# Seven products of w_up: partial sums kept growing in one pair of PSUM banks

## The chip, the cores and the metric

The kernel runs on one core of a Trainium2 chip. The metric is the device time of one execution in microseconds, lower is better; three runs of the kernel before are given, and one profiled execution.

## The reference

One layer of a streaming encoder in float32, for 1024 positions after 16 meta tokens, width 1024. Attention, a convolution module and their merge come first (some 1050 us of the kernel, not touched by the change); then a gated MLP whose two branches run through a causal convolution of three taps:

```python
n2 = _rms(h, norm_ffn_w[l])
up = _causal_dwconv(n2 @ w_up[l], ffn_dw_w[l], ffn_dw_b[l])     # w_up: 1024 x 5632
gate, val = jnp.split(up, 2, axis=-1)
h = h + (jax.nn.silu(gate) * val) @ w_down[l]                   # w_down: 2816 x 1024
out = _rms(h, norm_final_w)
```

## The kernel before

Activations lie with features on the partitions. Each factor of a product is split into two float32r parts, high and low, and `mm3` (line 141) makes three matmuls of each product of parts (lines 143 to 145): high by high, low by high, high by low.

w_up has 44 column tiles of 128: 22 of the gate and 22 of the value. Tiles p and 22 + p are made as a pair. The first two pairs go by plain products; the other twenty (p = 2 to 21) by Winograd's form of Strassen's algorithm in `strassen` (line 920): w's two tiles are cut into four blocks by halves of the features (a11, a12, a21, a22), the activations into four by halves of the features and of the tokens (b11, b12, b21, b22), and seven products of blocks and of sums of blocks give four results: c11 and c12 (the gate, in the row tile u1), c21 and c22 (the value, u2). The sums s1 to s4 of w's blocks are made per pair by `seven` (line 894) on VectorE; t1 to t4 of the activations are made once.

`product` (line 839) makes one of the seven: 24 matmuls with 258 columns each, 12 into either of two PSUM banks. `banks` gives a pair of banks from a pool of four such pairs, so all eight banks are used in turn. In the program's names, `ps_u` is such a pair, and the second factor names the product: `b11h`/`b11l` for a11 b11, `t2h`/`t2l` for s2 t2, `b21` for a12 b21, `t3` for s3 t3, `b12` for a22 t4 (t4 lies where b12 was), `t1` for s1 t1, `b22` for s4 b22. `whi` and `wlo` are the two parts of w's blocks, made by a cast on ScalarE (line 688) and a subtraction on VectorE (line 689).

Each product has banks of its own. The first is copied to u1 on ScalarE (line 928), and VectorE adds the other six to rows of u1 and u2 in SBUF, in seven additions (line 926), since s1 t1 goes into two results. Then `act` (line 831) runs the convolution of three taps over u2 and u1 (`conv3`: one step on ScalarE, line 825, and two on VectorE, line 827, for each row), the SiLU on ScalarE (line 835), the product of gate and value on VectorE (line 836), and stores the result. Rows u1, u2 and the convolution's two rows come from one pool of four (`urow`), so the next pair's u1 and u2 take places that the pair before must have let go.

w_down follows, again in seven products by groups; its first blocks are loaded into places that w_up's operands have let go.

The order of instructions on each engine is set by a scheduler from priorities. Each engine runs its own instructions strictly in that order; semaphores hold it where it needs another's result.

Of the kernel before, what the change touches and what calls it, by code (L numbers as in the profile page):

```python
# [10 lines left out]
F32R = mybir.dt.float32r  # L11
# [8 lines left out]
KT = 8                # feature tiles of the model width  # L20
WARM = 18
T = 1040              # 16 meta tokens and 1024 positions
NM = 16               # meta tokens
T0 = 14               # first token whose residual stream is needed
TN = T - T0           # 1026
# [4 lines left out]
FT = 22               # feature tiles of the gate (and of the value)  # L30
# [4 lines left out]
# A head's attention by units of work: v by tokens, scores, transposes, products with v, and the norm of the  # L35
# head before it.  A unit goes with half a bank of another product's passes.
# [15 lines left out]
LATE = 7                # the first head whose gate is computed after the last step  # L52
STATS_FROM, METAS_FROM = 8, 18          # units of the last head's attention
LATER = 1000            # what gives way: the convolution to the next step's work, a chunk's last scaling to the
                        # next chunk's sums
DIRECT = 2              # of w_up's tiles, pairs by plain products
W_LATER = 300           # the parts of a weight that is not used yet
GROUPS = [3, 4, 4]      # pairs of feature tiles that w_down's products sum over in PSUM
AHEAD, BEFORE = 5, 3    # steps whose parts are made ahead, and those of them before the last tile of w_up is done
# [3 lines left out]
def trunk_kernel(  # L63
    ctx: ExitStack,
    tc: tile.TileContext,
    x: bass.AP,         # [1040, 1024]     meta tokens and positions
    xT: bass.AP,        # [128, 8, 1040]   the same, feature-major
    w_in: bass.AP,      # [56, 128, 1024]  per column tile: [k within tile, (k tile, column)]
    w_co: bass.AP,      # [8, 128, 1024]
    w_o: bass.AP,       # [8, 128, 1024]  # L70
    w_up: bass.AP,      # [44, 128, 1024]
    w_dn: bass.AP,      # [22, 128, 1024]  rows of w_down
    lam4: bass.AP,      # [128, 4, 64]
    pvec: bass.AP,      # [128, 49]  norm_mix, norm_ffn, norm_final, ln_w, ln_b, dw_b (8 each), subln
    dww: bass.AP,       # [128, 8, 31]
    fdw: bass.AP,       # [128, 44, 3]
    fdb: bass.AP,       # [128, 44]
    out: bass.AP,       # [128, 8, 1024]
):
    nc = tc.nc  # L80
    # ------------------------------------------------------------ constants
# [28 lines left out]
    def load_w(src, later):  # L110
        """Column tile of a weight as its two float32r parts."""
        raw = wpool.tile([P, KT * P], F32, tag="wraw", name="wraw", bufs=2)
        nc.sync.dma_start(raw, src)
        hi = wpool.tile([P, KT, P], F32R, tag="whi", name="whi", bufs=3)
        lo = wpool.tile([P, KT, P], F32R, tag="wlo", name="wlo", bufs=3)
        rv = raw.rearrange("p (k c) -> p k c", k=KT)
        tc.cur_priority += later
        nc.scalar.copy(hi, rv)  # L118
        nc.vector.tensor_tensor(out=lo, in0=rv, in1=hi.bitcast(F32), op=ALU.subtract)  # L119
        tc.cur_priority -= later  # L120
        return hi, lo

    class Weights:
        """The column tiles in the order of their use, each loaded one use ahead."""
# [16 lines left out]
    def mm3(ps, lh, ll, rh, rl, start, stop):  # L141
        """ps += l^T r from the two parts of each operand."""
        nc.tensor.matmul(ps, lh, rh, start=start, stop=False)  # L143
        nc.tensor.matmul(ps, lh, rl, start=False, stop=False)  # L144
        nc.tensor.matmul(ps, ll, rh, start=False, stop=stop)  # L145
# [13 lines left out]
    def rstd(dst, src, eps, n):  # L159
        """dst = (src / n + eps) ** -0.5"""  # L160
# [3 lines left out]
    # =================================================== phase A: mixing inputs  # L164
# [18 lines left out]
    # ---- the tensor engine's clock rises while the first tokens arrive  # L183
# [4 lines left out]
    # ---- normalised tokens, transposed  # L188
# [41 lines left out]
    # ---- parameters  # L230
# [20 lines left out]
    subs = const([P, 1], "subs")      # (1 - lambda_init) * subln, halved for the tanh gate  # L251
# [6 lines left out]
    def gate(w, dst):  # L258
        """tanh(g / 2) of one feature tile; sigmoid(g) = (tanh(g / 2) + 1) / 2"""
# [7 lines left out]

    Z = CK - 1 - T0                       # tokens before the first one that the convolution sees

# [13 lines left out]
    def conv(i, u):  # L283
        """y[2n] = sum (a + b)_j o[n+j] + sum a_j (e - o)[n+j], y[2n+1] = sum (a + b)_j o[n+j]
        + sum b_j (e' - o)[n+j] with the even and odd samples e, o, e'[n] = e[n+1] and the even
        and odd taps a, b."""
# [23 lines left out]
    # q: rows [hi; lo] of either map.  k: each part twice.  # L310
# [52 lines left out]
    def inputs(i):  # L363
        """The column tiles of step i, half a bank of products at a time."""
# [30 lines left out]
    # ---- attention of one head  # L395
# [5 lines left out]
    # the meta keys' parts under one another, for one pass: v [hi; hi; lo] by a [hi; lo; hi]  # L401
# [8 lines left out]
    def attention(h, vt, kh, kl, qq, units=UNITS):  # L410
        """One head, a unit of work at a time."""
# [3 lines left out]
        def tokens(b):  # L415
            """v with the tokens on the partitions; b = 2 for the meta tokens"""
# [20 lines left out]
        def probs(j):  # L437
            """a = p0 - lam p1 over the keys that tile j of queries may see"""
# [53 lines left out]
        def turned(g, b):  # L492
            """block b (key tiles 2b and 2b + 1, or the meta keys) of the group's probabilities, keys
            on the partitions"""
# [51 lines left out]
    def norm():  # L546
        """the last head's outputs over their root mean square"""
# [11 lines left out]
    def together(main, side):  # L559
        """Both streams of work, a unit of the second for each of the first."""  # L560
# [15 lines left out]
    # ---- LayerNorm over the channels of the convolution: mean, centred values, scale  # L576
# [37 lines left out]
    # ---- the two meta queries, over the meta keys, all heads at once  # L614
    om = const([P, 2 * H], "om")      # their normalised outputs
# [75 lines left out]
    # ---- the rest of the LayerNorm, SiLU  # L691
# [9 lines left out]
    def layernorm():  # L701
        for k in range(KT):
# [3 lines left out]
            y = row("y")                      # back in the order of the tokens  # L706
# [10 lines left out]
    # =================================================== phase B: merge and output projection  # L717
    pb = ctx.enter_context(ExitStack())
    bp = pb.enter_context(tc.tile_pool(name="bp", bufs=1, side="right", reuse_waits="tile"))
    mh = bp.tile([P, KT, 2 + TN], F32R, tag="mh", name="mmh")       # two tokens more, for even halves  # L720
# [35 lines left out]
    # From here on by halves: KH feature tiles each, and the tokens that 512 outputs of the last convolution need  # L756
    # after two others, which a pair of banks holds as 2 x N (even).
# [13 lines left out]
    def block(pool, tag):  # L771
        """The two parts of one block (half of the features, half of the tokens) of n2 or of a sum of its blocks."""
        return [pool.tile([P, KH, TH], F32R, tag=tag + part, name=tag + part) for part in "hl"]

    def out_proj(t):
        """h1 and its norm's scale for half t of the tokens"""
# [16 lines left out]
    def normalise(t, *blocks):  # L793
        """n2 in the place of h1"""
# [19 lines left out]
    # =================================================== phase C: conv-gated MLP, w_up  # L814
# [398 lines left out]
```

## Time and profile before

| what | us |
|---|---|
| median of three runs | 1748.23 |
| lowest and highest of them | 1743.93, 1749.63 |
| span of the profiled execution, first to last instruction | 1740.7 |
| TensorE, VectorE, ScalarE busy in it | 1716.3, 1391.4, 849.6 |
| w_up's twenty pairs of seven products, about | 1110 to 1510 |
| w_down and the last norm, about | 1510 to 1741 |

The profile gives the span of the profiled execution and no other time of it; the runs' times also hold what lies before the first and after the last instruction. Busy time is the sum of an engine's instructions. TensorE's matmuls overlap, so how long one takes is read from start to start.

### The profile page before, as it was taken

To read this page: it belongs to the slowest core of one execution; us is meant where nothing else is said; L and a number is where in the kernel's file an instruction comes from. 1 tells how busy PE (TensorE), PEld (TensorE's weight loads), DVE (VectorE), ACT (ScalarE), POOL (GpSimd) and SP (SyncE) were. 2 spreads that over 40 slices of the span, in tenths; PEclk is the share of its full clock that TensorE was granted. 3 is DMA by queue.
4 is the path that set the end of the run, shared out by engine and by line. 5 is a ranking of instruction groups with operands and counts; after the bars stand their busy time and mean duration, and the time that the engine had idled before them with its cause. 6 is when DMAs were issued, how large, how long until landed. Compare 5 with 4: busy or idle time off the path is not lost.

```text
span 1740.7 us, 29030 instructions
## 1 busy us (share of the span) xinstructions
PE 1716.3 (99%) x11736; PEld 1651.5 (95%) x11736; DVE 1391.4 (80%) x2065; ACT 849.6 (49%) x1407; POOL 39.4 (2%) x75
## 2 busy tenths in 40 slices
PE   8999999999999999999999999999999999999997
PEld 6999999999999999998999999999999999988886
DVE  5679697978888797986357466998888888799997
ACT  6245565646464637565642245543334434353345
POOL 2020000000000000000000000000000000000010
PEclk9999999999999999999999999999999999999999
DMA  4323222141414141367648443322222221583622
GB/s 167 98 67 86 79 66 88 54 111 50 116 49 105 49 111 42 104 193 221 183 136 250 170 144 112 121 98 79 80 74 73 86 85 37 188 279 100 189 55 97
DMA packets 80710, 195.58 MB, mean 112 GB/s; under 512 B 8624, under 2 KB 26416, under 8 KB 80192
## 3 DMA queue, kind: packets, MB, share of 16 engines
q1 hardware_dynamic: 78416, 187.43, 33.8%
q0 software_dynamic: 2160, 6.29, 2.0%
q8 instruction: 92, 1.51, 0.4%
q14 instruction: 42, 0.34, 0.1%
HBM read 130.54 MB, written 40.93 MB: 99 GB/s over the span
## 4 chain that ended last, share of the span: by engine, by line
PE 89%; DMA 5%; DVE 3%; ACT 1%; issue 1%; SPq 0%; POOL 0%; DVEq 0%; ACTq 0%
PE ps_u L144 8%; PE ps_u L145 8%; PE ps_u L143 8%; PE ps_d L145 4%; PE ps_d L143 4%; PE ps_d L144 4%; PE ps_g L143 3%; PE ps_g L144 3%; PE ps_g L145 3%; PE ps_s L398 2%; PE ps_s L399 2%; PE pt L508 2%; PE ps_o L143 2%; PE ps_o L144 2%; PE ps_o L145 2%; PE ps_b L144 2%
## 5 line engine op out<-in xcount | busy, mean ns | idle before, releaser
L299 DVE SCALAR_TENSOR_TENSOR acc<-d,taps,acc 128x513 f32<-128x513 f32 x248 | 170.3, 746 | 0.5
L118 ACT CAST whi<-wraw 128x1024 fp32r<-128x1024 f32 x84 | 88.1, 1050 | 119.5 <-PE ps_o L144 31.4
L145 PE MATMUL ps_g<-xh,wlo 128*128 128x342 f32 x384 | 125.6, 327 | 0.0
L143 PE MATMUL ps_g<-xh,whi 128*128 128x342 f32 x384 | 124.9, 325 | 0.5 <-ACT tg L264 0.5
L143 PE MATMUL ps_d<-part 128*128 128x512 f32 (+1 forms) x324 | 123.9, 382 | 0.0
L144 PE MATMUL ps_d<-part 128*128 128x512 f32 (+1 forms) x324 | 122.8, 379 | 0.9 <-DVE part L981 0.9
L144 PE MATMUL ps_g<-xl,whi 128*128 128x342 f32 x384 | 123.7, 322 | 0.0
L145 PE MATMUL ps_d<-part 128*128 128x512 f32 (+1 forms) x324 | 123.4, 381 | 0.0
L926 DVE TENSOR_TENSOR u<-ps_u,u 128x516 f32<-128x516 f32 x140 | 94.7, 689 | 34.8 <-PE ps_u L145 34.3
L119 DVE TENSOR_TENSOR wlo<-wraw,whi 128x1024 fp32r<-128x1024 f32 x84 | 102.3, 1218 | 22.0 <-ACT whi L118 20.2
L1009 ACT CAST part<-raw 128x1024 fp32r<-128x1024 f32 x66 | 69.0, 1051 | 95.0 <-PE ps_d L145 73.9
L827 DVE SCALAR_TENSOR_TENSOR g<-u,fw,g 128x1024 f32<-128x1024 f32 x88 | 110.6, 1277 | 0.6
L299 DVE SCALAR_TENSOR_TENSOR acc<-u,tab,acc 128x513 f32<-128x513 f32 x120 | 88.5, 737 | 0.8
L981 DVE TENSOR_TENSOR part<-raw,part 128x1024 fp32r<-128x1024 f32 x66 | 80.0, 1218 | 5.0 <-ACT part L1009 4.4
L143 PEld LDWEIGHTS ps_g<-xh,whi 128*128 128x128 f32 x384 | 73.0, 190 | 1.2 <-ACT tg L264 0.8
L144 PEld LDWEIGHTS ps_d<-part 128*128 128x128 f32 x324 | 60.9, 188 | 13.6 <-DVE part L981 1.4
L143 PE MATMUL ps_o<-mmh,whi 128*128 128x258 f32 x256 | 72.5, 283 | 1.0 <-DVE sg L744 1.0
L145 PEld LDWEIGHTS ps_g<-xh,wlo 128*128 128x128 f32 x384 | 72.9, 190 | 0.3
L144 PEld LDWEIGHTS ps_g<-xl,whi 128*128 128x128 f32 x384 | 72.7, 189 | 0.4
L398 PE MATMUL ps_s<-kh,q 128*128 128x392 f32 (+5 forms) x224 | 72.7, 333 | 0.0
L145 PEld LDWEIGHTS ps_d<-part 128*128 128x128 f32 x324 | 60.8, 188 | 12.2
L144 PE MATMUL ps_o<-mml,whi 128*128 128x258 f32 x256 | 72.3, 283 | 0.0
(323 smaller groups left out, 6039.0 us busy)
## 6 DMA issues: line engine op xcount, KB each, us to landing
wraw<-in_w_in_dram SPq DMA_DIRECT2D x56, 512.0 KB, 3.4
wraw<-in_w_up_dram SPq DMA_DIRECT2D x44, 512.0 KB, 3.3
a_d<-g SPq DMA_DIRECT2D x22, 512.0 KB, 3.0
raw<-in_w_dn_dram SPq DMA_DIRECT2D x22, 512.0 KB, 6.5
raw<-a_d SPq DMA_DIRECT2D x22, 512.0 KB, 7.3
lnc<-conv_d SPq DMA_DIRECT2D x16, 513.0 KB, 4.1
wraw<-in_w_o_dram SPq DMA_DIRECT2D x16, 512.0 KB, 3.7
kh<-kh SPq DMA_DIRECT2D x24, 260.0 KB, 3.8
```

Of the source, the lines that this page charges most:

```text
L118: nc.scalar.copy(hi, rv)
L119: nc.vector.tensor_tensor(out=lo, in0=rv, in1=hi.bitcast(F32), op=ALU.subtract)
L143: nc.tensor.matmul(ps, lh, rh, start=start, stop=False)
L144: nc.tensor.matmul(ps, lh, rl, start=False, stop=False)
L145: nc.tensor.matmul(ps, ll, rh, start=False, stop=stop)
L299: nc.vector.scalar_tensor_tensor(out=out, in0=src[:, k:k + n], scalar=w, in1=add, op0=ALU.mult, op1=ALU.add)
L398: nc.tensor.matmul(ps, qs, kh[m][:, k0:k0 + n], start=True, stop=False)
L399: nc.tensor.matmul(ps, qs, kl[m][:, k0:k0 + n], start=False, stop=True)
L827: nc.vector.scalar_tensor_tensor(out=g, in0=u[:, :, 2 + k:2 + k + 512], scalar=fw[:, ct, k:k + 1], in1=g, op0=ALU.mult, op1=ALU.add)
L926: nc.vector.tensor_tensor(out=dst, in0=ps, in1=src, op=ALU.add)
L981: nc.vector.tensor_tensor(out=out, in0=x, in1=y, op=op)
L1009: nc.scalar.copy(hi, x)
```

## The change

The four products a11 b11, s2 t2, s3 t3 and a22 t4 are added up in one pair of banks (`one`): c11's first term is what stands there after the first product, then, each time with a copy to SBUF in between, what c12 needs of it after the second, c22 after the third, and c21 after the fourth. Two more, s1 t1 and s4 b22, share another pair (`two`), which is read once after s1 t1 (added to c22) and once after s4 b22 (added to c12); a12 b21 has a pair of its own. A product that goes on in its banks (`on=True`) starts without clearing them. Per pair of tiles ScalarE copies four times and VectorE adds three times, where it was one copy and seven additions. The products stand in another order in the code. `skip_group_check` concerns the build alone, and comments are taken out. The line numbers after the change are three higher at this place.

```diff
-    def mm3(ps, lh, ll, rh, rl, start, stop):
-        nc.tensor.matmul(ps, lh, rh, start=start, stop=False)
-        nc.tensor.matmul(ps, lh, rl, start=False, stop=False)
-        nc.tensor.matmul(ps, ll, rh, start=False, stop=stop)
+    def mm3(ps, lh, ll, rh, rl, start, stop, on=False):
+        nc.tensor.matmul(ps, lh, rh, start=start, stop=False, skip_group_check=on)
+        nc.tensor.matmul(ps, lh, rl, start=False, stop=False, skip_group_check=on)
+        nc.tensor.matmul(ps, ll, rh, start=False, stop=stop, skip_group_check=on)
...
-    def product(ps, *factors):
+    def product(ps, *factors, on=False):
...
-                        i == k == 0, i == len(factors) - 1 and k == KH - 1)
+                        i == k == 0 and not on, i == len(factors) - 1 and k == KH - 1, on)
...
-        nc.scalar.copy(c11, product(banks("ps_u"), (a11, b11)))
-        plus(c12, c11, product(banks("ps_u"), (s2, t2)))
-        plus(c11, c11, product(banks("ps_u"), (a12, b21)))
-        plus(c22, c12, product(banks("ps_u"), (s3, t3)))
-        plus(c21, c22, product(banks("ps_u"), (a22, t4)))
-        ps = product(banks("ps_u"), (s1, t1))
-        plus(c22, c22, ps)
-        plus(c12, c12, ps)
-        plus(c12, c12, product(banks("ps_u"), (s4, b22)))
+        one, two = banks("ps_u"), banks("ps_u")
+        nc.scalar.copy(c11, product(one, (a11, b11)))
+        plus(c11, c11, product(two, (a12, b21)))
+        nc.scalar.copy(c12, product(one, (s2, t2), on=True))
+        two = banks("ps_u")
+        product(two, (s1, t1))
+        nc.scalar.copy(c22, product(one, (s3, t3), on=True))
+        plus(c22, c22, two[:, :, :N])
+        plus(c12, c12, product(two, (s4, b22), on=True))
+        nc.scalar.copy(c21, product(one, (a22, t4), on=True))
```

The scheduler makes more of it than the code says. Before, a pair's products stand one behind the other on TensorE, in the order of the code; here, in the pair p = 8, the end of s3 t3 (banks 13478) and the start of a22 t4 (banks 13504):

```order
L144 MATMUL ps_u_13478<-t3l_11474,whi_13168 128x258
L145 MATMUL ps_u_13478<-t3h_11473,wlo_13169 128x258
L143 MATMUL ps_u_13504<-b12h_11960,whi_13172 128x258 [waits Activation_49]
L144 MATMUL ps_u_13504<-b12l_11961,whi_13172 128x258
L145 MATMUL ps_u_13504<-b12h_11960,wlo_13173 128x258 [waits DVE_49]
L143 MATMUL ps_u_13504<-b12h_11960,whi_13172 128x258
```

Of the change, at the same place, TensorE has six matmuls of the next pair's a11 b11 (banks 13587) between the two, which are now sums in one pair of banks (13370), and a22 t4 waits for ScalarE:

```order
L144 MATMUL ps_u_13370<-t3l_11474,whi_13143 128x258
L145 MATMUL ps_u_13370<-t3h_11473,wlo_13144 128x258
L143 MATMUL ps_u_13587<-b11h_10956,whi_13348 128x258 [waits PE_49]
L144 MATMUL ps_u_13587<-b11l_10957,whi_13348 128x258
L145 MATMUL ps_u_13587<-b11h_10956,wlo_13349 128x258
L143 MATMUL ps_u_13587<-b11h_10956,whi_13348 128x258
L144 MATMUL ps_u_13587<-b11l_10957,whi_13348 128x258
L145 MATMUL ps_u_13587<-b11h_10956,wlo_13349 128x258
L143 MATMUL ps_u_13370<-b12h_11960,whi_13147 128x258 [waits Activation_49]
L144 MATMUL ps_u_13370<-b12l_11961,whi_13147 128x258
L145 MATMUL ps_u_13370<-b12h_11960,wlo_13148 128x258 [waits DVE_49]
```

The order of a pair's 168 matmuls, from its b21 on, is now the same in 16 pairs (p = 5 to 20): 24 of b21, 13 of t1, 24 of t2 (waits for c11's copy), 11 of t1, 24 of t3 (waits for c12's copy), 6 of the next pair's b11, 7 of b12 (waits for c22's copy), 24 of b22 (waits for VectorE's addition to c22), 17 of b12, 18 of the next pair's b11. The pair p = 4 has 15 and 9 of t1 there; in the first two pairs there are 6 matmuls between t2 and t3 instead of 11; in the last one, which has no next pair, 4 matmuls of w_down stand between t3 and b12, and 5 of b12 ahead of b22.

On ScalarE before, the first product's copy (into u1_13398) stands behind the casts and steps of convolution (L825) of the pair ahead of it:

```order
L688 CAST whi_13172<-wraw_13152 128x512 [waits DMAHW7_49,PE_49]
L825 ACTIVATE g_13365<-u1_13176,fb_406,fw_404 128x2x512 [waits DMAHW3_49,DVE_49]
L928 COPY u1_13398<-ps_u_13400 128x516 [waits DVE_49,PE_49,Activation_49]
L835 ACTIVATE g_13365<-g_13365 128x2x512 [waits DVE_49]
L688 CAST whi_13384<-sa_13376 128x1024 [waits PE_49]
```

Of the change, at the same place on ScalarE, the pair ahead ends with a copy of its own (L939, c21), on which its convolution and with it the next pair's first copy (L931) follow:

```order
L688 CAST whi_13147<-wraw_13127 128x512 [waits DMAHW6_49,PE_49]
L939 COPY u2_13152<-ps_u_13153 128x516 [waits PE_49]
L825 ACTIVATE g_13331<-u2_13152,fb_406,fw_404 128x2x512 [waits DVE_49,Activation_49]
L825 ACTIVATE g_13335<-u1_13151,fb_406,fw_404 128x2x512 [waits DMAHW3_49,DVE_49]
L688 CAST whi_13354<-sa_13346 128x1024 [waits PE_49]
L931 COPY u1_13368<-ps_u_13370 128x516 [waits DVE_49,Activation_49]
L835 ACTIVATE g_13335<-g_13335 128x2x512 [waits DVE_49]
L933 COPY u1_13368<-ps_u_13370 128x516 [waits PE_49]
```

In both, VectorE's semaphore in the first copy's row is that of a step of the convolution of the pair ahead, the third of its four (L827) after the change; on VectorE the four now stand directly one behind the other, alternating between the value's and the gate's row.

## Rows read from the trace of the kernel before

**Rows 1.** The page's first lines: span, and TensorE's busy time.

```profile
span 1740.7 us, 29030 instructions
...
PE 1716.3 (99%) x11736; PEld 1651.5 (95%) x11736; DVE 1391.4 (80%) x2065; ACT 849.6 (49%) x1407; POOL 39.4 (2%) x75
```

**Rows 2.** Stretches: us, busy us (count) of PE, PEld, DVE, ACT, POOL; PEclk, DMA, GB/s.

```profile
1117.00:1500.00 383.00, 383.00 (x3192) 383.00 (x3191) 333.28 (x385) 151.35 (x154) 0.00 (x0) 1.00 0.21 75
1500.00:1515.00 15.00, 14.05 (x104) 13.14 (x103) 7.37 (x9) 5.68 (x6) 0.00 (x0) 1.00 0.98 355
1600.00:1741.00 141.00, 131.60 (x621) 109.74 (x619) 121.30 (x130) 62.71 (x79) 6.22 (x7) 0.98 0.41 120
```

**Rows 3.** What TensorE waited for: us in total, times, longest.

```profile
PE ps_d L144 <- DVE part L981: 0.9, 1, 0.9
```

**Rows 4.** TensorE's timeline at a product's end: start, us, instruction.

```profile
1265.26 0.28 PE L144 MATMUL ps_u<-t1l,whi 128*128 128x258 f32 x1
1265.38 0.28 PE L145 MATMUL ps_u<-t1h,wlo 128*128 128x258 f32 x1
1265.50 0.28 PE L143 MATMUL ps_u<-b22h,whi 128*128 128x258 f32 x1
```

**Rows 5.** ScalarE's timeline in the same pair; in brackets the idle time before.

```profile
1265.58 1.05 ACT L688 CAST whi<-wraw 128x1024 fp32r<-128x1024 f32 x1 [1.77 <-PE ps_u L144]
...
1272.44 0.59 ACT L928 COPY u<-ps_u 128x516 f32<-128x516 f32 x1 [1.82 <-DVE g L827]
1274.88 1.06 ACT L835 ACTIVATE g<-g 128x1024 f32<-128x1024 f32 x1 [1.84 <-DVE g L827]
```

**Rows 6.** VectorE's timeline in the same pair.

```profile
1269.26 1.27 DVE L827 SCALAR_TENSOR_TENSOR g<-u,fw,g 128x1024 f32<-128x1024 f32 x1
1270.45 0.68 DVE L689 TENSOR_TENSOR wlo<-wraw,whi 128x512 fp32r<-128x512 f32 x1
1271.05 3.79 DVE L827 SCALAR_TENSOR_TENSOR g<-u,fw,g 128x1024 f32<-128x1024 f32 x3
...
1275.97 1.23 DVE L836 TENSOR_TENSOR g<-g 128x1024 f32<-128x1024 f32 x1 [0.52 <-ACT g L835]
```

**Rows 7.** Groups by line, 1117 to 1500 us: count, busy us, mean ns.

```profile
L825 ACT ACTIVATE g<-u,fb,fw 128x1024 f32<-128x1024 f32 x38 | 47.3, 1245 | 16.5 <-DVE u L926 16.5
...
L928 ACT COPY u<-ps_u 128x516 f32<-128x516 f32 x20 | 11.8, 592 | 35.7 <-DVE g L827 35.4 <-PE ps_u L145 0.3
L688 ACT CAST whi<-wraw 128x512 fp32r<-128x512 f32 x19 | 11.8, 620 | 2.7 <-PE ps_u L144 0.7
...
L827 DVE SCALAR_TENSOR_TENSOR g<-u,fw,g 128x1024 f32<-128x1024 f32 x78 | 98.1, 1277 | 0.6
L926 DVE TENSOR_TENSOR u<-ps_u,u 128x516 f32<-128x516 f32 x135 | 91.3, 689 | 28.2 <-PE ps_u L145 27.8
```

**Rows 8.** Waits of the same stretch: ScalarE's first copy of a pair.

```profile
ACT u L928 <- DVE g L827: 35.4, 19, 2.7
```

**Rows 9.** A wait of TensorE for ScalarE: timeline of all engines (PEld loads weights).

```profile
842.60 0.32 PE L145 MATMUL ps_g<-xh,wlo 128*128 128x342 f32 x1
842.91 0.46 ACT L264 ACTIVATE tg<-ps_g 128x342 f32<-128x342 f32 x1
...
843.42 0.19 PEld L143 LDWEIGHTS ps_g<-xh,whi 128*128 128x128 f32 x1 [0.79 <-ACT tg L264]
843.42 0.42 PE L143 MATMUL ps_g<-xh,whi 128*128 128x342 f32 x1 [0.50 <-ACT tg L264]
```

**Rows 10.** ScalarE's timeline: two instructions without a wait between.

```profile
1519.66 1.06 ACT L835 ACTIVATE g<-g 128x1024 f32<-128x1024 f32 x1
1520.61 1.04 ACT L1009 CAST part<-raw 128x1024 fp32r<-128x1024 f32 x1
```

**Rows 11.** Timelines of ScalarE and TensorE at the start of w_down.

```profile
1509.24 1.05 ACT L1009 CAST part<-raw 128x1024 fp32r<-128x1024 f32 x1 [12.00 <-DMA raw<-a_d]
...
1514.54 0.50 PE L144 MATMUL ps_d<-part 128*128 128x512 f32 x1 [0.95 <-DVE part L981]
```

## The prediction

> **What bounds the kernel now.** I read the page's head first: TensorE is busy for 1716.3 of 1740.7 us [rows 1]. Matmuls overlap in this count, so the next view is the table of stretches. In the stretch in which w_up's twenty pairs of tiles are multiplied by seven products each, from 1117 to 1500 us, TensorE is busy for all 383 us, at full granted clock, with 3192 matmuls; VectorE for 333 us and ScalarE for 151 us [rows 2]. So a matmul with 258 columns takes 383 / 3192 = 0.120 us from start to start, and a pair, of 7 x 24 = 168 matmuls, 20.16 us. The timeline of TensorE shows the same pitch across the border of two products, here from t1 to b22: 1265.26, 1265.38, 1265.50 [rows 4]. The list of what TensorE waited for has no long wait in this stretch; the nearest is 0.9 us at the start of w_down, on VectorE [rows 3]. The stage is bound by TensorE's issue, with no gap that a change could close. The copies out of PSUM have slack instead: the first copy of a pair stands 1.8 us behind a step of the convolution [rows 5], 35.4 us over 19 pairs [rows 8], and TensorE doesn't notice, since the next three products write other banks.
>
> **The change, part by part.**
>
> *What it takes off the other engines.* Per pair VectorE loses four of seven additions (0.689 us each [rows 7]), 20 x 4 x 0.689 = 55 us; ScalarE gets three copies more (0.592 us each [rows 7]), 20 x 3 x 0.592 = 36 us. ScalarE goes from 151 to about 185 us of 383, VectorE from 333 to about 280. Neither is what ends this stage, so both count as nothing.
>
> *What stays.* The number of matmuls, their shapes and the loads of weights are the same; nothing comes off the 20.16 us.
>
> *What it adds: a wait for a copy ahead of a product.* The products a11 b11, s2 t2, s3 t3 and a22 t4 now grow in one pair of banks, so each of the last three may start only when the copy of what stood before is done. The order puts other products between them, and so most of each copy is covered. I work out each wait from the start of the last matmul before the copy, called 0, with these prices: TensorE to ScalarE 0.32 us from start to start (1265.26 [rows 4] to 1265.58 [rows 5]); ScalarE to VectorE 0.03 (1274.88 + 1.06 to 1275.97 [rows 5, 6]); VectorE to ScalarE 0.04 where one thing is waited for (1271.05 + 3.79 to 1274.88) and 0.11 where the copy of the first product waits for two (the first of three steps ends at 1271.05 + 1.28, the copy starts at 1272.44) [rows 5, 6]; ScalarE to TensorE 0.05 (842.91 + 0.46 to 843.42 [rows 9]). ScalarE starts an independent instruction 0.11 before its last one's end (1519.66 + 1.06 to 1520.61 [rows 10]), VectorE starts steps 1.19 apart (1269.26 to 1270.45 [rows 6]). And a matmul that waited takes 0.42 instead of 0.32, because its weights are loaded only then (both rows at 843.42 [rows 9]): 0.10 us on top of each wait.
>
> Before a22 t4: between it and s3 t3 stand 6 matmuls of the next pair. The copy c22 starts at 0.32 + 0.07 (it waits for two things), ends at 0.39 + 0.59 = 0.98, TensorE may go on at 1.03; the matmuls are through after 7 x 0.120 = 0.84. Wait 0.19, with the weights 0.29. The last pair has four longer matmuls of w_down there and doesn't wait: 19 x 0.29 = 5.5 us.
>
> Before s2 t2: the copy c11 of the next pair goes into the place of u1, u2 of the pair before, and so waits for that pair's convolution, which waits for the last copy, c21. What was slack is now on the path. From the last matmul of a22 t4: the cast of a weight that stands first on ScalarE waits for the matmul one before, 0.20; 0.62 long; c21 at 0.20 + 0.62 - 0.11 = 0.71 to 1.30; the convolution's first two steps on ScalarE (1.245 each) at 1.33 and 2.47, ending at 2.58 and 3.71; on VectorE three steps from 2.61, 1.19 apart, the third 1.28 long, to 6.27; c11 at 6.38 to 6.97; TensorE at 7.02. ScalarE's cast of the next pair's sums stands between, but waits only for b21 (5.24 to 6.29), so it is through. TensorE's work until then: 18 matmuls of b11, 24 of b21, 13 of t1, and the one at 0: 56 x 0.120 = 6.72. Wait 0.30, with the weights 0.40: 20 x 0.40 = 8.0 us. What queues up behind it is the whole of TensorE, so this shifts the pair.
>
> Before s3 t3: 0.32 + 0.59 + 0.05 = 0.96 against 12 x 0.120 = 1.44: covered by t1's other 11 matmuls. Only in the first two pairs, with 6 between, 0.12 + 0.10 each: 0.4 us. Without any cover it would be 0.84 + 0.10 in each pair, 19 us.
>
> Before s4 b22, in the second pair of banks: c22's addition on VectorE must have read s1 t1: 0.98 + 0.03 + 0.69 + 0.05 = 1.75, against 14 x 0.120 + 0.29 = 1.97: covered, but in the last pair about 0.1 + 0.1.
>
> *The start of w_down.* TensorE waits 0.95 us at 1514.54 for parts whose blocks were loaded late (ScalarE waits 12.0 us for them) [rows 11]. The blocks' places come free as w_up's last pair is done with b11 and b21, which now comes earlier against its end; but more of VectorE's work stands there. Between nothing left of it and twice as much: -1.1 to +1.1, taken as 0.
>
> **Sum.** 5.5 + 8.0 + 0.4 + 0.2 = 14.1 us on a span of 1740.7: 1754.8. The median of the runs shown, 1748.23, stands 7.5 us above the profiled span; with the same 7.5 the median of the changed kernel is 1762.3. I say 1762.5, 0.8% slower. Bounds: a hand-over 0.1 us shorter in each of the two waits of a pair takes away 39 x 0.1 = 3.9; if both are covered altogether the weights' 0.10 goes too, and it is the first rival. One that is 0.2 longer adds 7.8.
>
> With no other product between, the three waits would be 0.84 to 0.91 us, with the weights up to 1.01, in each of 20 pairs: 57 to 60 us, 1807. By the Trainium skill's "Perfetto Trace Analysis", section Matmuls, independent groups of matmuls should rotate through different PSUM banks so that the evacuation of one overlaps the matmuls of the next; the change gives this up for four products of seven, and by that rule alone the sum would be those 57 to 60 us. The rows agree with its sense (no wait in 383 us while the banks rotate [rows 2]). I stay with 14.1, since the order shows other products in between.
>
> **Rivals.**
>
> *Covered after all (chance 0.09).* If c11 starts 0.3 us earlier and c22 0.2 us, both waits vanish and 0.6 us is left: 1749. For it: both are small differences of long sums. Against: the pitch of 0.120 and the hand-overs are the same in every pair. One wait of the two alone gives 1754 or 1757, which I count with the forecast's lower end.
>
> *Copies late (0.13).* ScalarE takes its work in order. If an instruction in front of c12 or c22 has to wait for VectorE or a load, the copy is late by it, and TensorE now at once. For it: ScalarE stood 1.8 us behind a convolution's step before [rows 5], and c12 stands behind the SiLU, which waits for the convolution's last step. Against: that step ends at 6.27 + 1.19 = 7.46, the SiLU (1.06) at 8.6, and s2 t2 only at 7.02 + 0.10 + 2.88 = 10.0. A lateness of one more VectorE operation, 0.69 to 1.28 us, in each pair adds 14 to 26 us: 1776 to 1788. Its far end, no cover at all, is the 1807 above; it has 0.01 of the 0.13.
>
> *The clock falls (0.02).* If the new gaps let TensorE's clock go from 2.4 to 1.2 GHz, a matmul takes up to its pitch of 0.120 us longer; in a tenth of the 3360 matmuls that is 40 us, 1803. Against: around the 0.95 us wait at 1514 the granted clock is 1.00, and with 9.4 us idle in the last stretch 0.98 [rows 2]. This is the rule of the Trainium skill's "TensorE: Matmul & The Clock Gate", section "A second HAM failure mode: psum-queue depth-cycling": short idles between groups can make the clock swing. No row here shows such a swing for gaps of this size.
>
> *Faster (0.02).* If a product that goes on in the banks of another were cheaper than one that opens new ones, each of 60 such starts would save something; to win 5.3 us each would have to save 0.09 us and have no wait besides. Against: at a product's border the pitch is the same 0.12 as inside [rows 4]. VectorE's relief can give at most the 1.1 us at 1514.
>
> **Chances.** The forecast, waits of 0.2 to 0.6 us twice in a pair, has 0.74. Two runs of this kernel can be told apart from about 0.3%, 5.2 us. Slower by more: the forecast but its lowest edge, the late copies and the clock, 0.88; within: 0.10; faster: 0.02. The range from 1754 to 1776 leaves out the full cover, the clock, the gain and the larger half of the late copies, about 0.2.
>
> **What would show it.** Right: in the twenty pairs TensorE has two waits in each, before t2 (on the copy of c11, itself released by the convolution's step) and before a22 t4's b12 (on c22), some 0.3 and 0.2 us, and a pair takes 20.8 to 20.9 us; VectorE's share falls by about 55 us without effect. Wrong: no waits there and a pair of 20.16; or waits before t3 or b22, which I hold to be covered; or a granted clock under 1.00 in that stretch.

## The result, and the profile after

The changed kernel takes 1763.51 us in the median of 4 runs (1761.02 to 1767.48), the kernel before beside it 1746.08 us (1743.56 to 1749.63): a ratio of 1.0099, interval 1.0073 to 1.0124, so about 1% slower, 17.4 us. The forecast was 1762.5. Run again later, on a chip on which the kernel before takes 1743.84, it takes 1762.04, a ratio of 1.0102 (1.0089 to 1.0116).

First the page's head of the changed kernel, which answers to [rows 1].

```profile
span 1759.2 us, 28933 instructions
...
PE 1729.1 (98%) x11736; PEld 1655.6 (94%) x11736; DVE 1341.1 (76%) x1985; ACT 880.6 (50%) x1467; POOL 39.4 (2%) x75
```

TensorE has as many matmuls as before. VectorE has 50 us less to do, ScalarE 31 us more, and the span is 18.5 us longer. The same stretch of w_up as in [rows 2]:

```profile
1117.00:1500.00 383.00, 377.62 (x3064) 369.69 (x3063) 275.36 (x299) 174.36 (x203) 0.00 (x0) 1.00 0.21 76
```

In 383 us there are 3064 matmuls in place of 3192, at the same granted clock of 1.00. 128 matmuls of 0.120 us are 15.4 us that TensorE now spends in waits, where before it had none. What it waited for heads the list (us in total, times, longest):

```profile
PE ps_u L143 <- ACT u L931: 5.0, 19, 2.2
```

Line 931 is the copy of c11. The list counts from a matmul's modelled end, and so it shows less than is lost; the second wait of a pair is too short for it altogether. The timeline of TensorE has both, in one pair. First before t2:

```profile
1264.85 0.28 PE L143 MATMUL ps_u<-t1h,whi 128*128 128x258 f32 x1
1265.29 0.39 PE L143 MATMUL ps_u<-t2h,whi 128*128 128x258 f32 x1 [0.16 <-ACT u L931]
1265.52 0.28 PE L144 MATMUL ps_u<-t2l,whi 128*128 128x258 f32 x1
1265.64 0.28 PE L145 MATMUL ps_u<-t2h,wlo 128*128 128x258 f32 x1
```

From start to start it is 0.44 us where the pitch is 0.120: 0.32 lost. The matmul after it starts 0.23 later, another 0.11: the weights of the matmul that waited are loaded only as it starts, at 1265.29 (for the t1 matmul at 1264.85 they are loaded from 1264.73, 0.12 ahead), and those of the next one from 1265.39. Then before a22 t4:

```profile
1273.06 0.28 PE L145 MATMUL ps_u<-b11h,wlo 128*128 128x258 f32 x1
1273.36 0.39 PE L143 MATMUL ps_u<-b12h,whi 128*128 128x258 f32 x1
1273.58 0.28 PE L144 MATMUL ps_u<-b12l,whi 128*128 128x258 f32 x1
```

0.18 and 0.10 us here. ScalarE in the same pair (in brackets the idle time before):

```profile
1258.46 0.62 ACT L688 CAST whi<-wraw 128x512 fp32r<-128x512 f32 x1 [1.00 <-PE ps_u L144]
1258.99 0.58 ACT L939 COPY u<-ps_u 128x516 f32<-128x516 f32 x1
1259.60 2.38 ACT L825 ACTIVATE g<-u,fb,fw 128x1024 f32<-128x1024 f32 x2
1263.50 1.05 ACT L688 CAST whi<-sa 128x1024 fp32r<-128x1024 f32 x1 [1.52 <-PE ps_u L144]
1264.65 0.59 ACT L931 COPY u<-ps_u 128x516 f32<-128x516 f32 x1
...
1272.72 0.59 ACT L936 COPY u<-ps_u 128x516 f32<-128x516 f32 x1 [2.00 <-PE ps_u L145]
```

The last copy of the pair before, c21, ends at 1259.57. The convolution's steps follow on ScalarE and then on VectorE, 1.19 us apart from 1260.88:

```profile
1260.88 4.88 DVE L827 SCALAR_TENSOR_TENSOR g<-u,fw,g 128x1024 f32<-128x1024 f32 x4 [0.22 <-ACT g L825]
```

The third of these four ends at 1260.88 + 2 x 1.19 + 1.28 = 1264.54, and c11's copy starts at 1264.65 and ends at 1265.24. TensorE goes on at 1265.29. Every link of the chain in the prediction is there, from the cast at 1258.46 on. Now the first of the twenty pairs, TensorE, ScalarE and VectorE:

```profile
1117.71 0.28 PE L143 MATMUL ps_u<-b11h,whi 128*128 128x258 f32 x1
1120.16 0.39 PE L143 MATMUL ps_u<-t2h,whi 128*128 128x258 f32 x1 [2.17 <-ACT u L931]
```

```profile
1119.52 0.59 ACT L931 COPY u<-ps_u 128x516 f32<-128x516 f32 x1 [2.67 <-DVE g L827]
```

```profile
1113.31 1.90 DVE L689 TENSOR_TENSOR b12l<-h,b12h 128x516 fp32r<-128x516 f32 x3
1115.13 0.69 DVE L912 TENSOR_TENSOR sa<-wraw 128x512 f32<-128x512 f32 x1
1115.73 4.87 DVE L827 SCALAR_TENSOR_TENSOR g<-u,fw,g 128x1024 f32<-128x1024 f32 x4
```

Here 2.33 us are lost, not 0.3: VectorE is still at work on sums of blocks and their parts, and the four steps of the convolution, of which c11's copy waits for the third, start at 1115.73. I summed over w_up what lies beyond 0.120 us from one start to the next: before t2 2.33 in the first pair, 6.08 in the other 19, and 2.11 for the matmuls after; before b12 3.41 and 2.04; before t3 0.25 and 0.21, all in the first two pairs; before b22 0.11. Together 16.5 us. The other 2 us of the span lie ahead of w_up, where the code is the same: its first matmul starts at 1061.4 us, before at 1059.3, and in the twelve profiles of this study anywhere from 1058.0 to 1065.4. From that matmul to the end it is 697.8 us here and 681.3 before, 16.5 more. This length leaves out what differs ahead of w_up, and the experiments below are also read by it.

### The profile page after: what moved, and what is told of

Same layout as the page of the kernel before. It is cut to its first block, busy times and chain, and to the rows that moved or that the text cites. A ratio compares the mean times of both kernels' runs of the same rounds, so it can differ in the third digit from the quotient of the medians.

```text
span 1759.2 us, 28933 instructions
## 1 busy us (share of the span) xinstructions
PE 1729.1 (98%) x11736; PEld 1655.6 (94%) x11736; DVE 1341.1 (76%) x1985; ACT 880.6 (50%) x1467; POOL 39.4 (2%) x75
## 3 DMA queue, kind: packets, MB, share of 16 engines
q8 instruction: 92, 1.51, 0.4%
## 4 chain that ended last, share of the span: by engine, by line
PE 82%; DVE 7%; ACT 5%; DMA 3%; issue 3%; POOL 0%; SPq 0%; ACTq 0%; DVEq 0%
PE ps_u L143 6%; PE ps_u L144 5%; PE ps_u L145 5%; PE ps_d L145 4%; PE ps_d L143 4%; PE ps_d L144 4%; DVE g L827 3%; PE ps_g L143 2%; PE ps_g L144 2%; PE ps_g L145 2%; PE ps_s L398 2%; PE ps_s L399 2%; PE pt L508 2%; PE ps_o L144 2%; PE ps_o L143 2%
## 5 line engine op out<-in xcount | busy, mean ns | idle before, releaser
L928 DVE TENSOR_TENSOR u<-ps_u,u 128x516 f32<-128x516 f32 x60 | 41.6, 694 | 93.2 <-PE ps_u L145 62.7
L827 DVE SCALAR_TENSOR_TENSOR g<-u,fw,g 128x1024 f32<-128x1024 f32 x88 | 107.4, 1281 | 5.0 <-ACT g L825 4.9
L144 PEld LDWEIGHTS ps_d<-part 128*128 128x128 f32 x324 | 60.9, 188 | 13.7 <-DVE part L984 1.6
L145 PE MATMUL ps_o<-mmh,wlo 128*128 128x258 f32 x256 | 72.3, 283 | 0.0
```

The source lines that it names most:

```text
L144: nc.tensor.matmul(ps, lh, rl, start=False, stop=False, skip_group_check=on)
L145: nc.tensor.matmul(ps, ll, rh, start=False, stop=stop, skip_group_check=on)
L827: nc.vector.scalar_tensor_tensor(out=g, in0=u[:, :, 2 + k:2 + k + 512], scalar=fw[:, ct, k:k + 1], in1=g, op0=ALU.mult, op1=ALU.add)
L928: nc.vector.tensor_tensor(out=dst, in0=ps, in1=src, op=ALU.add)
```

## The experiments

**Theory W** is that of the prediction: the time is TensorE's waits for copies ahead of products that go on in the same banks, and its two steady waits come from the chain from c21 over the convolution to c11, and from the short cover of c22. Its rivals: that going on in a used pair of banks costs by itself; that ScalarE's added copies do; and that a wait is set by ScalarE's queue. Ratios are to the kernel before, whose median was 1742.76, 1745.29 and 1743.84 us in the three sets of runs. "Ratio x" is followed by its 95% interval.

**1. No copies between the products of the shared pair `one`.** Edit:

```diff
-        nc.scalar.copy(c11, product(one, (a11, b11)))
-        plus(c11, c11, product(two, (a12, b21)))
-        nc.scalar.copy(c12, product(one, (s2, t2), on=True))
+        product(one, (a11, b11))
+        nc.scalar.copy(c11, product(two, (a12, b21)))
+        product(one, (s2, t2), on=True)
...
-        product(two, (s1, t1))
-        nc.scalar.copy(c22, product(one, (s3, t3), on=True))
-        plus(c22, c22, two[:, :, :N])
-        plus(c12, c12, product(two, (s4, b22), on=True))
+        nc.scalar.copy(c22, product(two, (s1, t1)))
+        product(one, (s3, t3), on=True)
+        nc.scalar.copy(c12, product(two, (s4, b22), on=True))
```

> Left out: the copies of the sums between the products in the shared banks (only the last sum is copied, and two sums of the other pair of banks), so that no product of the shared banks has to wait for ScalarE; c11, c12 and c22 are then not the reference's. All four products still go on in one pair of banks. Theory W (the added time is TensorE's waits for the copies): no waits in w_up, a pair takes 20.16 us again, 1763.5 - 16.4 = about 1747. Rival B (to go on in the banks of another product costs by itself, at the reopened sums): the time stays at about 1763, pairs at 20.9 us. Rival S (ScalarE's added copies or the new order of the other engines' work make TensorE wait elsewhere): two of the three added copies are gone, so a third of the loss stays, about 1752.

Measured 1743.57 us, ratio 1.0002 (0.9993 to 1.0011).

```profile
1117.00:1500.00 383.00, 382.68 (x3186) 382.47 (x3185) 247.84 (x251) 174.65 (x210) 0.00 (x0) 1.00 0.22 78
```

3186 matmuls against 3192: the waits are gone, but for 0.48 + 0.11 us in the first pair, before b22, where the sum of s1 t1 is still copied out of `two` in between. With them all of the loss is gone, though four products still grow in one pair of banks; from w_up's first matmul on it is 681.2 us for 681.3. The edit keeps four copies in a pair, as many as the change has, where the expectation speaks of two fewer; so ScalarE is as busy as in the changed kernel and the rival of its load is out too. Going on in used banks costs nothing, and gives nothing. VectorE has another 28 us less in this stretch, without effect.

**2. The rows of the sums elsewhere.** Edit:

```diff
+        if away:
+            u = op0.tile([P, KH, TH], F32, tag="h1", name="u1")
+            u1, u2 = u[:, 0:2], u[:, 2:4]
+        else:
+            u1, u2 = urow("u1"), urow("u2")
...
+        us = strassen(ws, p % 2 and p < FT - 4)
```

> In 8 of the 20 pairs (each second one from pair 3 to 17) the rows of the sums, u1 and u2, lie in another place, so that from pair 3 to 18 the copy of c11 need not wait for the convolution of the pair before. Theory W with its chain: before t2 the wait goes in 16 pairs: c11's copy may start when ScalarE is done with the convolution's first steps, 3.7 us after the last matmul of a22 t4, and ends at 4.3; the matmuls until t2 are now 43, 5.2 us: covered. The waits before b12 stay, 0.18 us and the second matmul's 0.105. So 16 x 0.42 = 6.7 us less, about 1757. Rival C (the wait before t2 is set by ScalarE's queue or by the copy itself and not by the place that comes free): 1763 unchanged.

Measured 1752.93 us, ratio 1.0059 (1.0047 to 1.0072): against the changed kernel's 1.0102 (number 10) it is 7.5 us less, where 6.7 was expected. ScalarE shows the link that was cut:

```profile
1277.30 2.38 ACT L825 ACTIVATE g<-u,fb,fw 128x1024 f32<-128x1024 f32 x2
1279.58 0.57 ACT L935 COPY u<-ps_u 128x516 f32<-128x516 f32 x1
1281.19 1.05 ACT L688 CAST whi<-sa 128x1024 fp32r<-128x1024 f32 x1 [1.05 <-PE ps_u L144]
```

c11's copy (line 935 here) follows the convolution's first two steps at once, without waiting for VectorE's. Before t2 TensorE waits only in the first and the last three pairs; before b12 it still does in 19, in 16 of them for 0.12 us in place of 0.18. The chain by way of the place in memory is shown.

**3. Banks of its own for a22 t4.** Edit:

```diff
+        plus(c21, c22, product(banks("ps_u"), (a22, t4)))
         plus(c22, c22, two[:, :, :N])
         plus(c12, c12, product(two, (s4, b22), on=True))
-        nc.scalar.copy(c21, product(one, (a22, t4), on=True))
```

> Only a22 t4 gets banks of its own again and is added on VectorE; t2 and t3 still go on in the first product's banks, b22 in s1 t1's. Theory W: the wait before b12 is gone with its copy, and c21 is ready earlier against the next pair, with 72 matmuls (8.6 us) from the end of a22 t4 to t2, where the chain to c11's copy takes about 7 us: the wait before t2 goes too. Left are the first pair's 2 us and some tenths: 1747 to 1750. Rival B (each product that goes on costs by itself): two of three stay, about 1758.

Measured 1757.44 us, ratio 1.0080 (1.0066 to 1.0093): a miss, it gives back only some 4 us. By its number it would be rival B's 1758, but that rival needs a cost at t2 and t3 in every pair, and in the profile TensorE goes on to t2 in 19 pairs and to t3 in 19 without losing time; both steady waits are gone as expected. Each pair now waits before b22 for VectorE's addition instead, 0.065 us and 0.10 for the weights, 3.2 us in 19 pairs. The first pair keeps its 2.3. And w_down starts more slowly; TensorE there:

```profile
1522.68 0.50 PE L143 MATMUL ps_d<-part 128*128 128x512 f32 x1 [2.40 <-ACT part L1012]
1523.02 0.40 PE L144 MATMUL ps_d<-part 128*128 128x512 f32 x1
1523.25 0.39 PE L145 MATMUL ps_d<-part 128*128 128x512 f32 x1
...
1523.77 0.63 PE L144 MATMUL ps_d<-part 128*128 128x512 f32 x1
1524.20 0.63 PE L145 MATMUL ps_d<-part 128*128 128x512 f32 x1
```

After a wait of 2.4 us seven matmuls start 0.43 us apart, where the pitch just before and after is 0.23: the granted clock is 0.62 in 1524 to 1528. From w_up's first matmul on the profile has 692.2 us, 10.9 more than the kernel before: 2.4 in the first pair, some 1.5 of a fallen clock behind it (0.74 and 0.91 in the two stretches of 5 us from 1115), 3.2 before b22, and some 3 at the start of w_down. The expectation had only the first of these. The profiled run is the fastest of its six (1751.96 us), in part because its w_up starts earliest of the twelve profiles, at 1058.0. The others, 2 to 7 us longer, have a clock of 0.992 to 0.994 over the whole run against its 0.995; what else they contain stays open, since they left no trace.

**4. The kernel before with ScalarE's load.** Edit:

```diff
-        nc.scalar.copy(c11, product(banks("ps_u"), (a11, b11)))
+        ps = product(banks("ps_u"), (a11, b11))
+        for _ in range(4):
+            nc.scalar.copy(c11, ps)
```

> The kernel before, with the copy of c11 done four times in place of once: ScalarE has 60 copies (36 us) more, as in the change, and TensorE's order is that of before, with every product in banks of its own. Theory W: no product waits for these copies, so 1746 as before (within 2 us). Rival S (ScalarE's added load costs by itself): up to 1763.

Measured 1747.54 us, ratio 1.0024 (1.0012 to 1.0036), 4.2 us more by the ratio where within 2 was expected: a miss. In w_up the profile has a single wait that the kernel before lacks (the copy is line 930 here):

```profile
1124.18 0.39 PE L143 MATMUL ps_u<-b12h,whi 128*128 128x258 f32 x1 [2.07 <-ACT u L930]
```

It is in the first pair: b12 takes over the banks of b11, whose copies start late there. In the 19 others the added copies cost TensorE nothing. The wait is 2.2 of the 4.2 us, whose interval begins at 2.1. From w_up's first matmul on the profile has only 1.4 us more than the kernel before, since 0.9 less is spent behind w_up. What else is in the 4.2 stays open. So in w_up the added load costs TensorE nothing where the pairs run in step, but it does at the start of the stage, where VectorE is behind.

**5. Banks of its own for s4 b22.** Edit:

```diff
         plus(c22, c22, two[:, :, :N])
-        plus(c12, c12, product(two, (s4, b22), on=True))
+        plus(c12, c12, two[:, :, :N])
+        plus(c12, c12, product(banks("ps_u"), (s4, b22)))
```

> Only s4 b22 gets banks of its own and an addition of its own; t2, t3 and t4 still go on in the first product's banks. It need not wait for VectorE then, and the order puts its 24 matmuls between t3 and t4. Theory W: before b12 25 matmuls, 3.0 us, cover the 1.03 us to the end of c22's copy; and as nothing of the next pair stands ahead of t4 any more, 62 matmuls, 7.4 us, cover the 7.02 us from t4's end to c11's copy. Both steady waits go, 19 x (0.42 + 0.28) = 13.3 us, at the price of one addition more on VectorE, which has room: 1750 against 1763.5, ratio to before about 1.002; the first pair's 2.3 us are left. Rival L (the waits come back at another place, as they did with t4's own banks): about 1757, 1.006.

Measured 1754.78 us, ratio 1.0059 (1.0047 to 1.0072), where 1750 and 1.002 were expected: a miss, and near rival L's number. The wait before b12 is gone, as expected. The one before t2 is smaller, 0.10 us and 0.10 for the weights, but not gone, and ScalarE shows why:

```profile
1263.60 1.05 ACT L688 CAST whi<-sa 128x1024 fp32r<-128x1024 f32 x1 [2.24 <-PE ps_u L144]
1264.56 0.58 ACT L931 COPY u<-ps_u 128x516 f32<-128x516 f32 x1
```

By the convolution's third step, which ends at 1263.92, the copy of c11 could have started at 1264.03, but it stands behind a cast that waits for TensorE's matmuls on b21. As the convolution now leaves room, ScalarE's order is next in line: the rival of late copies, in a version where I had taken the cast to be through. It costs 18 x 0.20 = 3.6 us. The first pair still loses 2.3, and its clock falls besides (0.88 and 0.78 in the two stretches of 5 us from 1120).

**6 and 7. The first pair as before, in 5 and in the changed kernel.** Edit, and the call with `first = (p == DIRECT)`:

```diff
+        if first:
+            nc.scalar.copy(c11, product(banks("ps_u"), (a11, b11)))
+            plus(c12, c11, product(banks("ps_u"), (s2, t2)))
...
+            return u1, u2
         one, two = banks("ps_u"), banks("ps_u")
```

> As b22_own_banks, and the first of the twenty pairs is computed as in the kernel before (seven products in banks of their own). Theory W: no wait of over 0.1 us in w_up is left: 1747 to 1748 against 1763.5, ratio 1.000 to 1.001; nothing is won on before, since VectorE's saved additions were not on the path. Rival F (the four products in one pair of banks make TensorE faster or free VectorE for something on the path): under 0.997.

> The changed kernel with the first of the twenty pairs as in the kernel before. Theory W: the first pair's wait before t2, 2.33 us, and that before its t3, 0.23, go; the 19 other pairs stay: 1761 against 1763.5, ratio 1.0085. Rival K (the wait of 2.3 us lets TensorE's clock fall for some us in part of the runs, as the profiles of two other kernels show with 0.66 and 0.74 in 5 us): 2 us more, 1759, 1.007.

Measured 1750.02 us, ratio 1.0030 (1.0019 to 1.0041), and 1761.43 us, 1.0090 (1.0076 to 1.0104). Number 6 misses its 1.000 to 1.001, and number 7 comes near its 1.0085, though not as I thought: the first pair's 2.33 us are gone, but the wait is now in the second pair, 1.84 us in both, at a clock of 1.00. In number 6, 17 steady waits of 0.10 and 0.10 before t2 stay as well, as in number 5: 3.4 us. TensorE and VectorE of number 7 (c11's copy is line 942 there):

```profile
1137.80 0.39 PE L143 MATMUL ps_u<-t2h,whi 128*128 128x258 f32 x1 [1.68 <-ACT u L942]
```

```profile
1132.22 1.22 DVE L689 TENSOR_TENSOR wlo<-wraw,whi 128x1024 fp32r<-128x1024 f32 x1
1133.36 0.69 DVE L928 TENSOR_TENSOR u<-ps_u,u 128x516 f32<-128x516 f32 x1
1133.96 1.28 DVE L827 SCALAR_TENSOR_TENSOR g<-u,fw,g 128x1024 f32<-128x1024 f32 x1
1135.16 0.69 DVE L689 TENSOR_TENSOR wlo<-wraw,whi 128x512 fp32r<-128x512 f32 x1
1135.76 2.48 DVE L827 SCALAR_TENSOR_TENSOR g<-u,fw,g 128x1024 f32<-128x1024 f32 x2
```

VectorE goes from one instruction to the next without a gap, with parts of weights and additions ahead of the convolution that c11 waits for. The first pair's own additions are part of that work: as before there are seven of them, four more than in the changed kernel, whose second pair waits only 0.32. So the first pair that shares banks while VectorE is behind pays, and the edit lets VectorE stay behind for longer.

**8. The copy of c22 twice.** Edit:

```diff
-        nc.scalar.copy(c22, product(one, (s3, t3), on=True))
+        three = product(one, (s3, t3), on=True)
+        nc.scalar.copy(c22, three)
+        nc.scalar.copy(c22, three)
```

> The changed kernel with the copy of c22 done twice, one after the other (0.48 us more). The order of TensorE changes with it: b11 of the next pair stands ahead of t2 of this one, so that from the last matmul of a22 t4 to t2 there are only t1 and b11, 49 x 0.120 = 5.9 us, in place of 6.7. Theory W: the wait before t2 grows to 7.02 - 5.9 = 1.1 us, 19 x 0.8 = 16 us more; b12 has 12 matmuls, 1.44 us, against 1.51 to the end of the second copy, some 0.1 less wait than now: 1777 in all, ratio 1.018. Rival A (the longer copy adds its own length to the wait before b12): 19 x 0.48 = 9, 1772.5, 1.015. Rival N (waits for copies don't matter): 1763.

Measured 1790.11 us, ratio 1.0250 (1.0234 to 1.0266): 26.6 us above 1763.5 where 13.5 were expected, a miss.

```profile
1256.14 0.28 PE L145 MATMUL ps_u<-b11h,wlo 128*128 128x258 f32 x1
1257.42 0.39 PE L143 MATMUL ps_u<-t2h,whi 128*128 128x258 f32 x1 [1.00 <-ACT u L931]
```

The wait before t2 is 1.28 - 0.12 = 1.16 us in 14 pairs, where the chain gave 1.1 for 19. The rest of the sum was short: b12 waits as before (0.19 to 0.20), t3 now waits 0.12 and 0.10 in most pairs, since c12's copy stands behind a cast,

```profile
1260.48 1.05 ACT L688 CAST whi<-wraw 128x1024 fp32r<-128x1024 f32 x1 [1.50 <-PE ps_u L144]
1261.44 0.58 ACT L933 COPY u<-ps_u 128x516 f32<-128x516 f32 x1
```

and the last pair waits 2.75 us before t2 and 1.51 before b12. The 23 us by which its waits in w_up exceed those of the changed kernel (39.9 for 16.4) are nearly two thirds the wait before t2 (23.2 for 8.4); some 3 us are the granted clock, which fell in the first pair and in the last. The order of products in front of a wait decides its size, not the length of the copy alone.

**9. All three removed:** the edits of 2, 5 and 6 together.

> Banks of its own for s4 b22, the first of the twenty pairs as in the kernel before, and the rows of every second pair from 3 to 17 in another place. t2, t3 and t4 still go on in the first product's banks in 19 pairs. Theory W: c11's copy waits neither for the convolution nor behind the cast of the sums, so t2 finds its banks copied in all pairs up to 18; in the last three 0.1 us and 0.1 for the weights stay: under 1 us in all, ratio to before 1.000 to 1.001. Rival V (VectorE is behind at the start of the stage, whatever the first pair does, and the wait of 1.8 us only moves on to another pair): 1.002 to 1.003. Rival F (VectorE's saved additions are worth something as soon as the waits are gone): under 0.997.

Measured 1743.72 us, ratio 1.0001 (0.9992 to 1.0010).

```profile
1117.00:1500.00 383.00, 382.83 (x3183) 382.33 (x3183) 297.14 (x330) 176.82 (x208) 0.00 (x0) 1.00 0.22 80
```

This one computes all that the kernel before does, with three additions less per pair, and 19 pairs with four products in one pair of banks. With the convolution off c11's path, b22 ahead of t4, and the first pair out of it, TensorE waits 0.85 us in all, in the last three pairs; from w_up's first matmul on it is 681.5 us for 681.3. The kernel ties with the kernel before and doesn't beat it: VectorE's saved 38 us (1353.8 against 1391.4 busy) are worth nothing.

**10. The changed kernel again.**

> The changed kernel itself beside the others on one chip, for the distance between them. Theory W: 1.0099 as at first, with the clock in the first pair's wait as the uncertain part: 1.009 to 1.011. Rival: another chip and other runs give another distance, so that differences of 2 to 3 us between the experiments mean nothing: outside 1.008 to 1.012.

Measured 1762.04 us, ratio 1.0102 (1.0089 to 1.0116). The waits are those of the first profile, to 0.1 us. One thing differs; the stretch behind the first pair's wait, here and, below, in the first profile:

```profile
1120.00:1125.00 5.00, 4.08 (x22) 4.08 (x23) 5.00 (x7) 1.65 (x2) 0.00 (x0) 0.69 0.17 61
```

```profile
1120.00:1125.00 5.00, 4.84 (x38) 4.67 (x39) 5.00 (x7) 2.65 (x4) 0.00 (x0) 1.00 0.08 29
```

Here the granted clock fell from 2.4 to 1.2 GHz for a part of these 5 us: 16 matmuls more than in the first profile started about 0.22 apart in place of 0.12, 1.5 us.

## Why the prediction was right, by its own steps

**What bounds the kernel: right.** TensorE's issue bounds w_up. Numbers 1 and 9 give the time of before to 0.1% with 89 and 38 us less for VectorE than [rows 1] (1302.6 and 1353.8 against 1391.4), and number 4 shows no wait of TensorE for the added copies in w_up outside the first pair. The page has 50 us less for VectorE and 31 more for ScalarE where the prediction had 55 and 36, in part because busy time counts once what neighbouring instructions overlap; neither is a term of the sum.

**The wait before b12: right.** 5.5 us forecast, 3.41 + 2.04 = 5.45 measured: 0.18 and 0.10 in 19 pairs for 0.19 and 0.10.

**The wait before t2: right in 19 pairs, short in one.** 0.32 + 0.10 was measured for 0.30 + 0.10, in every steady pair, and number 2 shows that the path is the one named. The term failed in the first pair, which was priced like the others at 0.40 and took 2.43: the prices of the convolution came from a pair in step [rows 6], but in the first pair the convolution of the last plain pair stands behind other work on VectorE, which is busy without a gap from 1105 to 1125 us. The 8.0 us were 10.5. That it is the backlog, and not something in the first pair's sharing of banks, numbers 6 and 7 show: with the first pair as before, which keeps VectorE behind for longer, the second one waits 1.84 us. In number 9, where the second pair's rows lie elsewhere besides, this wait is gone.

**Before t3 and b22: right.** 0.46 us for 0.4, in the first two pairs alone; 0.11 for 0.2, in the last.

**The start of w_down: right.** TensorE waits there more often but shorter; from w_up's last matmul to the end it is 0.8 us less than before, and four of w_down's matmuls stand ahead of that last one (0.9 us): 0.1 in sum.

**The sum and the median.** The waits were 16.5 us for 14.1. The distance of the medians is 17.4, and 18.2 in number 10. The forecast of the time came out closer than its sum: the 7.5 us by which the median was taken to stand above the profiled span was 4.3 in the changed kernel, and the waits short by 2.4 and the later start of w_up, 2.1 us, which is no part of the change, went the other way. That the median was met to 1.0 us is luck; the sum was 2.4 short.

**The rivals.** Full cover is out for this order, and number 9 shows what it takes. Copies late behind ScalarE's queue did not happen in the changed kernel, but in numbers 5 and 8, as soon as the order left it to ScalarE. The clock did fall, but in the first pair alone, and not in each execution: in the changed kernel 1.5 us in one profile and nothing in the other, not 40. By the Trainium skill's "Perfetto Trace Analysis", section Matmuls, independent groups of matmuls should rotate through different banks so that an evacuation overlaps the next group. The traces agree in sense. What is lost, by the waits measured here, is not the copies but what other products fail to cover of them: 16.5 us and not 57 to 60, and 0.85 in number 9.

## What to carry to other kernels

Where several products grow in one pair of banks, each copy between them becomes a wait of TensorE unless the order puts as many other matmuls there as the copy's whole chain takes; count them from the order, and follow the chain back to the memory that the copy writes into, which is here what the convolution held. A steady pattern priced from one pair says nothing of the first one: look there at how far behind the other engines are. And relief for an engine that nobody waits for is worth nothing, however much it is.

## What the runs showed of the hardware

A matmul that waited lost about 0.10 us more than its wait, in each of some 40 waits of the changed kernel: its successor starts 0.22 us behind it where the pitch is 0.12; even a wait of 0.065 us (number 3) costs that.

In w_up and at the start of w_down, the granted clock fell behind some of the longest waits of TensorE: in the first pair of five of the seven profiles with a wait of 2.2 to 2.3 us there (0.66 to 0.91 in a stretch of 5 us), in number 3 after 2.4 us at the start of w_down, and in number 8 around the 2.75 us in the last pair. It cost 1.5 to 1.7 us where I counted it. In the other two of the seven, the changed kernel's first profile and number 4, it stayed at 1.00. Behind the waits of 1.7 us in numbers 6 and 7 it stayed at 1.00 as well, and behind the steady waits of 0.2 to 0.4 us it did too. By the Trainium skill's "TensorE: Matmul & The Clock Gate", section "A second HAM failure mode: psum-queue depth-cycling", short idles between groups can make the clock swing. With idles of 0.2 to 1.2 us, twice in each 21 us, no profile here shows it.
